# A two-layer conditioned decoder trunk on one core: two adaLN vectors moved from TensorE to VectorE rows, bf16 fillers spread through the norms, weight splits and a tanh pinned later

## The chip, the cores and the metric

The kernel runs on one NeuronCore of one Trainium2 chip. The metric is the device time of one execution in microseconds (us); several executions are timed and the median is given. Beside them stands one profiled execution, with its own time and the span from its first to its last instruction. PE is TensorE, DVE is VectorE, ACT is ScalarE, POOL is GpSimd, and SP is the queue from which all weight transfers are issued.

## The reference, cut to what matters

Two layers are computed on 256 tokens of width 1024, in float32. Each layer takes six vectors of 1024 from a conditioning vector `c`, which does not depend on the tokens:

```python
c_act = jax.nn.silu(c)
for l in range(DEPTH):
    # six vectors of layer l, r = 0..5
    sh1, sc1, g1, sh2, sc2, g2 = split(c_act @ w_mod[l] + b_mod[l], 6)
    h = modulate(rms_norm(x, mix_norm_g[l]), sh1, sc1)     # h*(1+sc)+sh
    x = x + g1 * token_mixer(h, ...)                       # MLA, MoBA, conv, gates, w_out
    h = modulate(rms_norm(x, ffn_norm_g[l]), sh2, sc2)
    x = x + g2 * channel_mixer(h, w_up[l], ..., w_down[l]) # conv over 3 tokens, silu(a)*b
```

Below, (l, r) is vector r of layer l: (0, 5) is the gain `g2` of layer 0, (1, 2) is `g1` of layer 1 and (1, 3) is `sh2` of layer 1. Each such vector needs a 1024 x 1024 matrix, 4 MB, that is read once.

## The kernel before, in words

Everything lies transposed: 128 partitions by 8 tiles of 256 tokens. Each large product is made of three float32r matmuls on halves of both operands (`flush`, L304 to L321): high by high, high by low, low by high. Weights come in units of 128x1024 float32 (512 KB). Each unit is loaded by SP (`wload_unit`, L218), then split into a high half by ACT (L232) and a low half by DVE (L233). `take` (L281) hands out the units in the order of use. It loads and splits up to three units beyond those asked for (`AHEAD` = 3), and four buffers of each kind rotate.

A planner of the compiler orders each engine's instructions by the order in which the program traces them and by when their operands are ready; an instruction that is ready early can stand well ahead of its place in the program. `tc.issue_after(i)` puts the instructions of its block that run on the engine of `i` behind `i`. After that each engine works its list in order.

The six vectors of each layer are made in one of two ways:

- as a part on TensorE (`mod_part`, L415 to L437): eight loads of 512 KB; for each, four matmuls with `c` as a 32-column stationary operand (L424, seen as eight records); then a copy, two transposes (L432) and an addition (L434);
- as rows on DVE (`mod_row`, `use_row`, L405 to L413): eight loads of 512 KB, each multiplied with `c` laid out along a row and summed in the same instruction (L407), then an addition of one column (L408).

Before, (0, 5) and (1, 3) are parts. They serve as filler in the two norms that stop the matmul stream: the norm ahead of the feed-forward block of layer 0 (called the first norm below), and the norm at the head of layer 1 (the second norm). There the eight residual updates (L1290, L1462) are followed by squares on ACT (L546), sums of pairs on DVE (L554), matmuls with a column of ones (L559), mean plus epsilon (L536), a power of -0.5 on POOL (L537), two transposes that spread the result (L569), and then eight tiles, each in three steps: L615 on DVE, L616 on ACT for the high half, L617 on DVE for the low half. The feed-forward or projection matmuls can begin with the first tile. `norm_stats` (L572) puts bf16 matmuls on constant ones (`warm`, L336) in between: 4, 7 and 3 of them.

Rows of (1, 0), (1, 1) and (1, 2) run during the feed-forward block of layer 0, those of (0, 3), (0, 4) and (1, 4) late in the two token mixers, and those of (1, 5) in the feed-forward block of layer 1. `c` is laid out as a row once more in each mixer: a load, a tanh on ACT (L1262) and a product on DVE (L1263).

The order of the mixers is written out by hand in `STEPS` (L76). In the late part, `G` are gate projections, `O` and `OC` output projections, `PR` the final projection, `RW0` to `RW3` make the row of `c`, and `r0`, `r1` mark the stretch over which rows are spread. The order of the feed-forward block comes from `_ffn` (L134): how many `up` steps run before the first `down` step. An `up` step is two units and its convolution (L1422 to L1433); `acts` are its high and low halves, the operands of `down`.

## Time and profile before

| | |
|---|---|
| median of 3 runs | 902.07 us (900.52 to 902.74) |
| profiled execution, its own time | 905.0 us |
| its span | 902.9 us |
| busy: PE, DVE, ACT, POOL | 881.3, 807.8, 556.9, 50.7 us |
| transfers | 201.59 MB, 223 GB/s in the mean |

In the rows of a timeline the first number is the start in us, the second the time in us until the last of the merged instructions ended, then engine, line, operation, out<-in with shapes, and how many instructions are merged; a bracket tells how long the engine had been idle and what ended that. A row of a group view has count, busy time and the mean of one in ns. A row of the windows view has a stretch, its length, and the busy time with count of PE, PEld (weight loads), DVE, ACT and POOL, then the granted clock, the share of busy DMA engines, and GB/s. Matmul ends are modelled: a float32r matmul of 256 columns shows 0.28 us but the next one starts 0.113 us after it.

### The profile page before, as it was taken

The page shows a single profiled execution, that of the slowest core. Times are in us where ns is not written, and L with a number is a line of the kernel's source. Part 1 is how long each engine was busy: PE and PEld are TensorE (multiplying, and loading weights), DVE is VectorE, ACT ScalarE, POOL GpSimd, SP SyncE. Part 2 cuts the span into 40 slices and gives each one's busy share as a digit, 9 for nine tenths or more (in the row PEclk, how much of TensorE's full clock was granted, in tenths as well). Part 3 has the DMA queues.
Part 4 walks back from the last instruction along what each step waited for, and adds up shares of the span by engine and source line. Part 5 has one row for each costly group of instructions (what it writes and reads, how often), then busy time and mean ns, then how long its engine had stood idle before and what let it go on. Part 6 is the DMA issues. An engine that isn't in the chain of part 4 may idle for free.

```text
span 902.9 us, 18611 instructions
## 1 busy us (share of the span) xinstructions
PE 881.3 (98%) x7247; PEld 836.2 (93%) x7247; DVE 807.8 (89%) x1592; ACT 556.9 (62%) x998; POOL 50.7 (6%) x36
## 2 busy tenths in 40 slices
PE   8999899999999999999999999999999999999998
PEld 6888788998997999999999988989999999999998
DVE  6989899999988999999875999999987899998774
ACT  4677579744666655556543676788465777556551
POOL 1010710000000000000000034000000000000000
PEclk8999999999999999999999999999999999999999
DMA  8956615598998989997752656157866575987631
GB/s 320 376 202 198 196 59 176 183 318 304 318 315 283 332 273 326 301 318 236 214 176 76 202 184 209 53 164 232 264 205 211 163 232 176 308 281 211 194 95 48
DMA packets 57976, 201.59 MB, mean 223 GB/s; under 512 B 6944, under 2 KB 8480, under 8 KB 57888
## 3 DMA queue, kind: packets, MB, share of 16 engines
q1 hardware_dynamic: 57888, 200.41, 66.9%
q8 instruction: 57, 0.93, 0.4%
q14 instruction: 31, 0.25, 0.1%
HBM read 199.33 MB, written 1.05 MB: 222 GB/s over the span
## 4 chain that ended last, share of the span: by engine, by line
PE 76%; DVE 13%; ACT 4%; DMA 4%; issue 2%; SPq 0%; POOL 0%; DVEq 0%; ACTq 0%; POOLq 0%
PE psb L316 15%; PE psb L317 15%; PE psb L319 15%; PE psa L316 7%; PE psa L317 7%; PE psa L319 7%; DVE wlo L233 4%; DVE cacc L1142 2%; ACT whi L232 2%; DVE raw L817 1%; PE psa L424 1%; PE psa L735 1%; PE psa L747 1%; PE psa L680 1%; DMA raw<-in_win 1%
## 5 line engine op out<-in xcount | busy, mean ns | idle before, releaser
L232 ACT ACTIVATE whi<-raw 128x1024 fp32r<-128x1024 f32 (+2 forms) x286 | 295.4, 1041 | 173.7 <-PE psb L317 90.7
L233 DVE TENSOR_TENSOR wlo<-raw,whi 128x1024 fp32r<-128x1024 f32 (+2 forms) x286 | 340.0, 1194 | 48.2 <-ACT whi L232 40.5
L316 PE MATMUL psb<-hh,whi 128*128 128x256 f32 x1056 | 254.7, 282 | 0.6 <-ACT p L714 0.3
L317 PE MATMUL psb<-hl,whi 128*128 128x256 f32 x1056 | 252.3, 279 | 0.0
L316 PEld LDWEIGHTS psb<-hh,whi 128*128 128x128 f32 x1056 | 198.6, 188 | 5.5 <-issue 3.3
L317 PEld LDWEIGHTS psb<-hl,whi 128*128 128x128 f32 x1056 | 198.8, 188 | 0.5 <-DVE wlo L233 0.4
L319 PE MATMUL psb<-hh,wlo 128*128 128x256 f32 x1056 | 144.2, 278 | 0.0
L319 PEld LDWEIGHTS psb<-hh,wlo 128*128 128x128 f32 x1056 | 131.0, 188 | 0.8 <-issue 0.8
L1142 DVE SCALAR_TENSOR_TENSOR cacc<-upad,cw,cacc 128x256 f32<-128x256 f32 x240 | 105.9, 479 | 0.4
L316 PE MATMUL psa<-mhl,whi 128*128 128x256 f32 x400 | 93.3, 277 | 0.0
L317 PE MATMUL psa<-mhl,whi 128*128 128x256 f32 x400 | 93.1, 276 | 0.0
L537 POOL TENSOR_TENSOR rs<-rs,mhalf 128x8 f32<-128x8 f32 (+3 forms) x26 | 49.1, 1900 | 674.4 <-DVE rs L536 674.4
L1424 DVE SCALAR_TENSOR_TENSOR e<-psb,fw,e 128x255 f32<-128x255 f32 (+1 forms) x168 | 79.8, 476 | 4.3 <-ACT e L1422 3.7
L316 PEld LDWEIGHTS psa<-mhl,whi 128*128 128x128 f32 x400 | 74.9, 188 | 0.0
L317 PEld LDWEIGHTS psa<-mhl,whi 128*128 128x128 f32 x400 | 74.9, 188 | 0.0
L1422 ACT ACTIVATE e<-psb,fb,fw 128x256 f32<-128x256 f32 x84 | 46.5, 554 | 37.3 <-DVE e L1424 34.7
L407 DVE SCALAR_TENSOR_TENSOR raw<-raw,crow 128x1024 f32<-128x1024 f32 x56 | 68.1, 1215 | 0.0
L319 PE MATMUL psa<-mhl,wlo 128*128 128x256 f32 x400 | 53.5, 276 | 0.0
L319 PEld LDWEIGHTS psa<-mhl,wlo 128*128 128x128 f32 x400 | 49.1, 188 | 0.0
L1432 ACT ACTIVATE mhl<-e 128x256 fp32r<-128x256 f32 x44 | 18.4, 417 | 43.6 <-DVE e L1430 42.1
L316 PE MATMUL psb<-whi,hh 128*128 128x416 f32 (+1 forms) x96 | 30.8, 349 | 3.2 <-ACT hh L893 3.1
L317 PE MATMUL psb<-whi,hl 128*128 128x416 f32 (+1 forms) x96 | 29.6, 343 | 0.2 <-DVE hl L894 0.2
(295 smaller groups left out, 1522.9 us busy)
## 6 DMA issues: line engine op xcount, KB each, us to landing
raw<-in_wup SPq DMA_DIRECT2D x88, 512.0 KB, 4.9
raw<-in_wmr SPq DMA_DIRECT2D x68, 512.0 KB, 5.4
raw<-in_wdn SPq DMA_DIRECT2D x44, 512.0 KB, 4.6
raw<-in_wgab SPq DMA_DIRECT2D x32, 512.0 KB, 4.9
raw<-in_wqkv SPq DMA_DIRECT2D x24, 512.0 KB, 4.8
raw<-in_wm SPq DMA_DIRECT2D x24, 512.0 KB, 4.4
raw<-in_win SPq DMA_DIRECT2D x16, 512.0 KB, 4.5
raw<-in_wgc SPq DMA_DIRECT2D x16, 512.0 KB, 4.1
```

The costliest lines, as they stand in the source:

```text
L232: ac.activation(hi, raw, AF.Copy)
L233: ve.tensor_tensor(lo, raw, hi.bitcast(F32), op=ALU.subtract)
L316: te.matmul(o, p1[0], p1[1], start=start, stop=False)
L317: te.matmul(o, p2[0], p2[1], start=False, stop=False)
L319: last = te.matmul(o, p3[0], p3[1], start=False, stop=stop)
L407: ve.scalar_tensor_tensor(raw, raw, scale, row, op0=ALU.mult, op1=ALU.mult, accum_out=acc)
L424: te.matmul(acc[32 * c:32 * c + 32, 0:S], cact[:, k:k + 1].to_broadcast([P, 32]), raw[:, c * S:(c + 1) * S], start=(k == 0), stop=(k == KD ...
L537: gp.tensor_tensor(r, r, mhalf[:, :n], op=ALU.pow)
L1142: ve.scalar_tensor_tensor(aj, upad[:, j, t:t + S], cw[:, j * 31 + t:j * 31 + t + 1], aj, op0=ALU.mult, op1=ALU.add)
L1422: ac.activation(t, src, AF.Identity, scale=fw[:, 2, c:c + 1], bias=fb[:, c:c + 1])
L1424: ve.scalar_tensor_tensor(t[:, d:S], src[:, 0:S - d], fw[:, 2 - d, c:c + 1], t[:, d:S], op0=ALU.mult, op1=ALU.add)
L1432: ac.activation(mh, th, AF.Copy)
```

## The change

- (0, 5) and (1, 3) are no longer parts on TensorE but rows on DVE. Their rows and those of (1, 2) are placed anew: 27 rows in the feed-forward block of layer 0 ((1, 0), (1, 1), (0, 5) and three of (1, 2)), one for each `up` step from the third on and two from the 13th to the 19th, each behind the low half of two `up` steps earlier; eight rows in the input projection of layer 1 (five of (1, 2), three of (1, 3)), behind the last tile; and the last five rows of (1, 3) in the late mixer of layer 1, in a new stretch `r2` to `r3`. The stretch `r0` to `r1` of (1, 4) ends earlier.
- The two norms have 5, 3, 9 and 7 bf16 fillers, placed ahead of the third and of the fourth pair of ones-matmuls, behind the fourth, and behind the transposes.
- The last unit taken before each of these norms is loaded but not split. It is split behind the last square (ACT) and behind the low half of the fourth tile (first norm) or of the third (second norm). In the input projection of layer 1 tiles are traced three ahead, and each split stands behind the newest tile. The instructions of the first two `up` steps of layer 0 stand behind the eighth tile (`MARK` = 7), where it was the second.
- The tanh that makes the row of `c` stands behind the last attention's high output half (L750).
- In layer 0 four `up` steps come before the first `down` step, where it was three.

```diff
-F1 = 2
-MARK = 1
+MARK = 7
+LATER = 1
+TWO_ROWS = range(12, 19)
+GATE_ROWS = {4: [(2, 3), (2, 4)], 5: [(2, 5), (2, 6)], 6: [(2, 7), (3, 0)], 7: [(3, 1), (3, 2)]}
-WARM1 = (4, 7, 3)
+WARM1 = (5, 3, 9, 7)
-ROWS = [(0, 0), (0, 1), (1, 0), (1, 1), (1, 2), (1, 5)] + RPARTS
+ROWS = [(0, 0), (0, 1), (0, 5), (1, 0), (1, 1), (1, 2), (1, 3), (1, 5)] + RPARTS
...
-    "OC0 G70 OC1 PR0 OC2 OC3 PR1 OC4 OC5 G71 O6 O7 PR2 OC6 PR3 OC7 PR4 r1 PR5 PR6 PR7 "
+    "r1 OC0 G70 OC1 r2 PR0 OC2 OC3 PR1 OC4 OC5 G71 O6 O7 r3 PR2 OC6 PR3 OC7 PR4 PR5 PR6 PR7 "
...
-FFN = [_ffn(2, 3), _ffn(4, 4)]
+FFN = [_ffn(3, 3), _ffn(4, 4)]
...
+    def split_rest(keep=0):
+        while len(raws_in) > keep:
+            raw, lead, ks = raws_in.pop(0)
+            ready.append((split(raw, lead), raw.shape[1] // len(ks), ks))
...
-            ready.append((split(wload_unit(src), lead), src.shape[1] // len(ks), ks))
+            raws_in.append((wload_unit(src), lead, ks))
+            split_rest(later[0])
...
-    def norm_stats(fill=None):
-
-        step(fill or iter(()), F1)
-        bank = psb() if sum(WARM1) else None
+    def norm_stats():
+
+        bank = psb()
...
-        if fill:
-            with tc.issue_after(last.ins):
-                step(fill, KD - F1)
...
+    def split_behind(mark):
+        hold[0] = [squares[0].ins, mark.ins]
+        split_rest()
+        hold[0] = None
...
+            with ExitStack() as es:
+                if n == 8 and k > 3:
+                    with tc.issue_after(last.ins):
+                        es.enter_context(tc.issue_after(warm(bank, WARM1[k // 2 - 2]).ins))
+                elif n == 8:
+                    es.enter_context(tc.issue_after((last if k > 1 else newest[0]).ins))
...
-        fill = mod_part(1, 3, ("oal", "obl", "vb", "lh0", "lh1", "lh2")) if l == 1 else None
...
         for k in range(KD):
             if l > 0:
-                norm_tile(k, bc, gs1[:, k:k + 1], sh1[:, k:k + 1], hh, hl)
+                if k + 3 < KD:
+                    tile(k + 3)
+                hold[0] = [i.ins for i in tiles[-1]]
                 conv_in(k)
-                mod_row(crow1[0], l, 2, k, scale=0.5 if CDMA else 1.0)
+                hold[0] = None
+                for n, (r, i) in enumerate(GATE_ROWS.get(k, ())):
+                    with tc.issue_after(tiles[-1][1].ins):
+                        mod_row(crow1[0], l, r, i, (SPARE[2 * (k % 2) + n], 1), 0.5 if CDMA else 1.0)
...
-                ac.activation(th, crow1[0], AF.Tanh, scale=0.5)
+                with tc.issue_after(heads[0].ins):
+                    ac.activation(th, crow1[0], AF.Tanh, scale=0.5)
...
-            fill = mod_part(l, 5)
-            bc = norm_stats(fill)
+            bc = norm_stats()
             hh, hl = new_h()
-            marks = [norm_tile(k, bc, gs2[:, k:k + 1], mod[l][:, 24 + k:25 + k], hh, hl) for k in range(KD)]
+            for k in range(KD):
+                marks.append(norm_tile(k, bc, gs2[:, k:k + 1], mod[l][:, 24 + k:25 + k], hh, hl))
+                if k == 3:
+                    split_behind(marks[k][1])
...
-        rows_left = [(1, r, k) for r in ((5,) if l else range(2)) for k in range(KD)]
+        rows_left = [(n, r, k) for n, r in (((1, 5),) if l else ((1, 0), (1, 1), (0, 5))) for k in range(KD)]
+        rows_left += [] if l else [(1, 2, k) for k in range(3)]
...
-                mod_row(crow1[0], *rows_left.pop(0), scale=0.5 if CDMA else 1.0)
+                row_next()
+                if not l and j in TWO_ROWS:
+                    row_next()
...
+        def row_next():
+            with tc.issue_after(parts[-3].ins):
+                mod_row(crow1[0], *rows_left.pop(0), scale=0.5 if CDMA else 1.0)
```

More of the change, by code (lines that the diff above doesn't have):

```diff
@@ L293, in take1 @@
         return take()[0][0][1]
-    queue = []
+    queue, newest = [], [None]
     def mmw(o, w, v, start, stop):
@@ L311, in flush @@
                 te.matmul(o, p2[0], p2[1], start=False, stop=False)
-                te.matmul(o, p3[0], p3[1], start=False, stop=stop)
+                newest[0] = te.matmul(o, p3[0], p3[1], start=False, stop=stop)
             queue.clear()
-            return None
+            return newest[0]
         for o, p1, p2, _, start, _ in queue:
@@ L552, in sq_sums @@
                 continue
-            else:
-                ve.tensor_tensor(one, one, sq, op=ALU.add)
-                if SQ4 and n == 4 and k < 3:
-                    continue
-            with tc.issue_after(warm(bank, WARM1[0]).ins) if bank is not None and WARM1[0] and k == n - 1 else ExitStack():
+            ve.tensor_tensor(one, one, sq, op=ALU.add)
+            if n == 4 and k < 3:
+                continue
+            with ExitStack() as es:
[4 more added lines that the diff above has]
+                    es.enter_context(tc.issue_after((last if k > 1 else newest[0]).ins))
                 for b in range(NB):
                     last = te.matmul(st[:, b:b + 1], one[:, b * P:(b + 1) * P], ones,
-                                     start=(k == (3 if SQ4 and n == 4 else 1) and b == 0),
-                                     stop=(k == n - 1 and b == 1))
+                                     start=(k == (3 if n == 4 else 1) and b == 0), stop=(k == n - 1 and b == 1))
         return st[:, 0:NB], last
@@ L907, in layer @@
             hold[0] = None
-        step(fill or iter(()))
         ahead[0] = AHEAD
@@ L1229, in project @@
                 acc.extend(psa() for _ in range(4))
+            if j == KD - 2 and l == 0:
+                later[0] = LATER
             if j % 2 == 0:
                 wor[:] = [u[0][1] for u in take(2)]
+            later[0] = 0
             for n in range(KD):
@@ L1307, in layer @@
         gs2 = mod_gain(l, 4, "ffn_g")
-        pre, marks, fill = [], [], None
+        pre, marks = [], []
         if l == 0:
@@ L1388, in down @@
                 acc2.extend(psa() for _ in range(4))
+            if j == NF - 1:
+                later[0] = LATER
             w = take1()
+            later[0] = 0
             for n in range(KD):
@@ L1455, in layer @@
                 up(j)
-            if j == 1 and fill:
-                step(fill)
         raw_tags[:] = [("raw", 4)]
```

43 lines of the change are left out of this document (26 added, 17 removed).

## The prediction

> **What bounds the kernel now.** I read the page first, then PE's timeline around the two norms, then the windows view for DVE's free time, then the rows of the tanh. The page's first part says who is full.
>
> ```profile
> span 902.9 us, 18611 instructions
> PE 881.3 (98%) x7247; PEld 836.2 (93%) x7247; DVE 807.8 (89%) x1592; ACT 556.9 (62%) x998; POOL 50.7 (6%) x36
> ```
>
> PE is busy almost throughout, so time is won only where PE is busy with something that is not needed, or pauses. One such place is the first norm. PE's timeline there:
>
> ```profile
> 277.63 0.28 PE L311 MATMUL psa<-mhl,whi 128*128 128x256 f32 x1
> 277.74 0.28 PE L312 MATMUL psa<-mhl,wlo 128*128 128x256 f32 x1
> ...
> 282.80 0.43 PE L569 MATMUL psb<-ident,rs 128*128 128x128 f32 x2 [0.31 <-POOL rs L537]
> ...
> 283.49 1.93 PE L424 MATMUL psa<-raw,cact 128*32 128x256 f32 x32
> 285.35 0.38 PE L316 MATMUL psb<-hh,whi 128*128 128x256 f32 x1
> ...
> 287.77 0.64 PE L424 MATMUL psa<-raw,cact 128*32 128x256 f32 x8
> 289.56 0.64 PE L424 MATMUL psa<-raw,cact 128*32 128x256 f32 x8
> ```
>
> The first two rows give the pace of useful work: one matmul every 0.113 us (to two digits 0.11), a unit of 24 in 2.72 us. The projection's last one starts at 277.74, the feed-forward block's first at 285.35, 7.6 us later, and fill (L424) stands ahead of it and twice inside the block that follows. What the block had done by 292.30, shown by the windows view for writers of the tile `psb` alone:
>
> ```profile
> 285.30:292.30 7.00, 5.81 (x46) 1.00 0.86 301
> ```
>
> It had 46 matmuls. The chain that brings the first tile runs over DVE and ACT (DVE's rows, then ACT's):
>
> ```profile
> 278.46 1.22 DVE L233 TENSOR_TENSOR wlo<-raw,whi 128x1024 fp32r<-128x1024 f32 x1
> 279.59 0.48 DVE L1290 SCALAR_TENSOR_TENSOR x<-psa,g1h,x 128x256 f32<-128x256 f32 x1
> 283.26 1.26 DVE L615 SCALAR_TENSOR_TENSOR e<-x,gs,psb 128x256 f32<-128x256 f32 x3 [1.37 <-PE psb L569]
> 283.78 0.91 ACT L616 ACTIVATE hh<-e,mod 128x256 fp32r<-128x256 f32 x2 [3.20 <-DVE e L615]
> ```
>
> A weight split stands ahead of the last residual update, whose operand PE had finished at 277.74 + 0.28 = 278.02. It holds the chain up by 279.59 - 278.46 = 1.13 us. The second norm has the same form (PE, DVE, then one ACT row):
>
> ```profile
> 468.15 0.28 PE L312 MATMUL psa<-mhl,wlo 128*128 128x256 f32 x1
> 473.46 2.80 PE L424 MATMUL psa<-raw,cact 128*32 128x256 f32 x48
> 476.19 0.38 PE L316 MATMUL psa<-hh,whi 128*128 128x256 f32 x1
> 469.25 1.22 DVE L233 TENSOR_TENSOR wlo<-raw,whi 128x1024 fp32r<-128x1024 f32 x1
> 470.39 0.42 DVE L554 TENSOR_TENSOR e<-e,e 128x256 f32<-128x256 f32 x1
> 473.24 1.26 DVE L615 SCALAR_TENSOR_TENSOR e<-x,gs,psb 128x256 f32<-128x256 f32 x3 [1.40 <-PE psb L569]
> 474.43 1.27 DVE L617 SCALAR_TENSOR_TENSOR hl<-e,mod,hh 128x256 fp32r<-128x256 f32 x3
> 468.98 0.87 ACT L546 ACTIVATE e<-x 128x256 f32<-128x256 f32 x2 [0.21 <-DVE x L1462]
> ```
>
> PE could have begun with the first low half at 474.43 + 0.42 = 474.85, but fill held it until 476.19.
>
> **The change part by part.** The sum is made against the profiled execution, 905.0 us with its span of 902.9; the median of the three runs is 902.07, and I carry the difference over to it unchanged.
>
> *First norm.* Without the split the chain is 1.13 us earlier: L615 starts at 282.13, the first high half is ready about 0.95 us after that (283.78 - 283.26 and one of the two ACT tiles), and PE can start near 283.1. Then tiles set the pace: by L615 (1.26 for three) and L617 (1.27 for three) a tile takes DVE about 0.8 us, eight take 6.6, and with the one held split (1.13) and the four small tap copies (some 0.4) the last low half is there near 290.3. Three units, 8.2 us of work, are at hand meanwhile, since the third is split behind the fourth tile. Dense from 284.1 on, they would be done by 292.3: 72 matmuls where the rows show 46, 26 x 0.113 = 2.95 us ahead. I take 2.4, since PE needs more than the first four tiles only late, but surely waits some 0.5 us for tiles in the first unit. The bounds are 1.1 (only the split goes; the tiles hold PE afterwards) and 2.95. Holding the first two steps behind the eighth tile costs nothing as long as the three units last: the next high half can be made by 291.3, and PE asks for it at 292.3. If a tile is late by more than that 1 us, PE waits.
>
> *Second norm.* The last sum waits for the split until 470.39; its square is ready at 468.98 + 0.87 = 469.85, so 0.5 us goes. Without fill PE starts its stream at 474.85 instead of 476.41 (one matmul after 476.19), another 1.56. Together 2.1; here a unit needs one tile only, 2.72 us of PE against 0.8 of DVE, so tiles do not hold PE. Bounds: 0.5, and 0.5 + 2.73 (473.46 to 476.19) = 3.2, were all of the fill in the way. The fillers that replace it, 9 behind the last pair of ones-matmuls (1.0 us) and 7 behind the transposes (0.8), fit into the waits there: from 282.80 + 0.43 to the first tile is just about 1 us.
>
> *The rest of the parts.* Each part has two transposes in the middle of the stream later:
>
> ```profile
> L432 PE MATMUL psa<-ident,e x6: 270/273/328, 254.8 to 498.5; 128*128 128x128 f32 x6
> L424 PE MATMUL psa<-raw,cact 128*32 128x256 f32 x192 | 14.5, 386 | 0.1
> L407 DVE SCALAR_TENSOR_TENSOR raw<-raw,crow 128x1024 f32<-128x1024 f32 x56 | 68.1, 1215 | 0.0
> ```
>
> Four of these six go: between 0.4 (0.11 each) and 1.1 us (0.27 each); I take 0.5. Of the 192 fill records 128 go, but their PE time lies in the two norms and is counted there.
>
> *The rows.* Sixteen rows are new. A row is 1.215 us and 0.08 for reading the sum and adding the column: 1.29, so 20.6 us of DVE. The loads stay sixteen of 512 KB on SP, since a row takes the place of a part's load; where a row's load waits for its buffer, weight loads queue behind it on SP. None of this lies on PE's path if DVE and the queue have room where it is put. Room is read from the windows view (the fifth column is DVE):
>
> ```profile
> 350.00:415.00 65.00, 65.00 (x575) 65.00 (x574) 65.00 (x126) 35.45 (x54) 0.00 (x0) 1.00 0.92 312
> 476.00:500.00 24.00, 24.00 (x211) 23.81 (x204) 11.25 (x20) 9.73 (x17) 0.00 (x0) 1.00 0.31 87
> 580.00:600.00 20.00, 19.68 (x190) 18.41 (x186) 20.00 (x40) 16.39 (x40) 0.00 (x0) 1.00 0.34 107
> 660.00:680.00 20.00, 20.00 (x179) 20.00 (x178) 17.13 (x30) 14.82 (x25) 0.00 (x0) 1.00 0.66 209
> 680.00:700.00 20.00, 20.00 (x178) 20.00 (x178) 15.59 (x27) 11.55 (x19) 0.00 (x0) 1.00 0.63 202
> ```
>
> In layer 0's feed-forward block DVE is full from 350 to 415, where two rows run for each `up` and `down`, and yet PE does not pause: 65.00 of 65.00. Afterwards 27 rows stand there instead of 24, but over all steps, and at most two for each step, for seven steps. Their transfers, 0.92 of the engines' time in that window, also stay at two for each step. Cost 0. The first four `up` steps in a row with a row in two of them may cost a little; I put 0.3 (0 to 1). The eight rows in the input projection need 10.3 us of the 12.75 that DVE has free from 476 to 500. What spills over delays the stretch behind it, where DVE is full (580 to 600). I put 0.3 (0 to 3). Their transfers come at a time when the DMA engines are a third busy (0.31): 0. The five in the late mixer need 6.5 of the 7.3 us that are free from 660 to 700. Queued behind such a row stand a split or the halves of a merged tile, and the projection on PE waits for those. The three units of reserve hide one row, not two in succession: 0.8 (0 to 6.5, all of them).
>
> *The tanh.* In layer 1 it stands ahead of the last attention's exponentials on ACT (L714), whose bias (L701) is done earlier; the rows below are ACT's, DVE's and PE's:
>
> ```profile
> 610.61 1.06 ACT L1262 ACTIVATE th<-crow 128x1024 f32<-128x1024 f32 x1
> 612.04 0.47 ACT L714 ACTIVATE p<-psa,nb,rs 128x128 f32<-128x128 f32 x1
> 627.52 1.06 ACT L232 ACTIVATE whi<-raw 128x1024 fp32r<-128x1024 f32 x1 [2.89 <-PE psb L317]
> 611.51 0.16 DVE L701 SCALAR_TENSOR_TENSOR nb<-mx,rs 128x4 f32<-128x4 f32 x1
> 635.35 0.67 PE L1155 MATMUL psb<-e,mean_w 128*128 128x256 f32 x2 [0.50 <-DVE mod L408]
> ```
>
> The exponentials could start 612.04 - 611.67 = 0.4 us earlier. The product and the first row follow the tanh to behind the attention, which frees 2.5 us of a full DVE; PE's pause of 0.5 us at the convolution's mean (635.35) may go. Behind the attention the 1.06 us of the tanh stand ahead of weight splits on ACT, but there ACT was idle for 2.89 us (627.52): 0. Together at most 1.0, and nothing if PE's other work fills these gaps anyway; I take 0.5. In layer 0 I put nothing.
>
> Sum: -2.4 - 2.1 - 0.5 - 0.5 + 0.3 + 0.3 + 0.8 = -4.1 us. The profiled execution goes from 905.0 to 900.9, the median from 902.07 to 898.0. 0.3% of the median is 2.7 us, about what a measurement of this kernel can tell from no change: faster means under 899.4, slower over 904.8.
>
> **The rivals.** *The gain is half taken back.* PE's starts move as forecast, but the first norm gives only its lower bound (1.1), as tiles hold PE, and the late rows cost two and a half of five (3.2): -1.1 - 2.1 - 1.0 + 0.6 + 3.2 = -0.4, 901.7, no change. For it: the first unit needs four tiles, 3.3 us of DVE, for 2.72 us of PE. Against it: two units can use these four tiles.
>
> *DVE becomes the bound of layer 1.* Thirteen new rows, 16.8 us, go into a layer where DVE is full at 580 to 600 and PE loses time. The two holes together have 12.75 + 7.3 = 20 us. If only a third can be used, since a row stands in the queue ahead of what PE needs, 16.8 - 6.7 = 10.1 us come onto the path: with -5.5 from the terms other than rows, and the 0.3 of layer 0, that is +4.9, 907.0, slower. It decides from the point on where less than 8.9 us of the holes serve (-5.5 + 0.3 + 7.9 = +2.7, and 16.8 - 7.9 = 8.9). Against it: the rows of the input projection stand where PE reads units split well ahead, and the planner puts unpinned rows into DVE's gaps.
>
> *The clock falls.* The granted clock is 1.00 in all windows above, that from 285.30 behind the first norm among them; the longest pause of PE in that norm shows as 0.31 us idle (282.80). With the fill gone, 24 fillers of 0.113 are 2.7 us of a norm of some 5.5; pauses of up to 1 us come back ahead of the last pairs. Were the clock to be halved over the first unit, each of its 24 matmuls would cost 0.113 more: 2.7 for each norm, 5.4 in all, 903.4, no change. The Trainium skill, "TensorE: Matmul & The Clock Gate", Part 1, says that the array falls back to half clock after an idle window of about 3.4 us; by that rule it does not happen here, and the trace agrees so far as a pause of 0.31 us left the clock at 1.00.
>
> *The change does not do what it says:* `issue_after` orders, it does not reserve. If the planner fills DVE's or ACT's queue in the norm with something else (a row, a step's convolution), both norms keep 1 us less each: -2.1, 900.0, no change.
>
> **How the numbers follow.** Forecast 0.60; half taken back 0.16; other work in the norms 0.08; the clock 0.03; DVE as the bound 0.13. So faster 0.60, no change 0.27, slower 0.13. The best sum takes every bound in favour: -2.95 - 3.2 - 1.1 - 1.0 = -8.2, 893.9; I start the range at 894.0. At the other end it takes in the cases of no change up to 903.5. Outside lie the 0.13 of the slower case and a few hundredths of the clock's.
>
> **What would show it.** Right: L316 starts some 5.5 us after the last L312 of the first norm, where it was 7.6, and some 6.0 after that of the second, where it was 8.0; no L233 between L1290 or L1462 and L536; from 290 to 460 no pause on PE; rows L407 right behind the last L617 of layer 1, done before the next stretch's convolution. Wrong: PE waits for L233 or L617 for over 1 us after the eighth tile; pauses at the projection of layer 1 that end with `mhl`; a granted clock under 1.00 behind a norm.

## The result and the profile after

The changed kernel takes 908.57 us (median of 6 runs, 906.48 to 910.27), the kernel before, on the same chip, 901.3 us (6 runs, 899.75 to 902.74). The ratio is 1.0079, with a 95% interval of 1.0058 to 1.0100: slower by 7 us, where I had forecast 4.1 us faster.

The profiled execution of after took 908.17 us, with a span of 906.0. That is only 3.1 above the span of before that the prediction quotes, and this number is not to be trusted: the profiled execution of before had an accident. Its rows, from PE's and POOL's timelines:

```profile
93.86 9.44 POOL L537 TENSOR_TENSOR rs<-rs,mhalf 128x16 f32<-128x16 f32 x2 [0.24 <-DVE rs L536]
106.95 0.28 PE L317 MATMUL psb<-hl,whi 128*128 128x256 f32 x1
110.30 2.08 PE L678 MATMUL psa<-qkT 96*128 96x128 f32 x8 [3.08 <-ACT qkT L1124]
```

Two powers on POOL took 9.44 us there. before_again is a second profile of the same kernel.

> The kernel before, unchanged, for a second profile. If the pause of 3.35 us at 106.7 and the slow matmuls behind it belonged to that one execution alone, they are gone and the span is near 897 us; if they are the kernel's ordinary course, they are there again and the span is near 903; half as much would say that the timed executions differ among themselves in this.

Four such powers take 10.60 us there, PE does not pause (the windows view has it busy for 23.86 of 24 us from 100 to 124), and the span is 897.5:

```profile
89.76 10.60 POOL L537 TENSOR_TENSOR rs<-rs,mhalf 128x16 f32<-128x16 f32 x4 [21.34 <-DVE rs L536]
```

From here on every kernel is laid against before_again. After is 906.0 - 897.5 = 8.5 us longer, which fits the 7.3 of the medians. The page's first part and the chain of after:

```profile
span 906.0 us, 18397 instructions
PE 876.4 (97%) x7135; PEld 835.9 (92%) x7135; DVE 827.9 (91%) x1638; ACT 557.1 (61%) x996; POOL 48.6 (5%) x36
PE 51%; DVE 30%; DMA 8%; ACT 5%; issue 5%; SPq 0%; POOL 0%; DVEq 0%; ACTq 0%; POOLq 0%
```

DVE has 20 us more to do (827.9 against 807.8), and the chain that ended last now runs over DVE and transfers for 38% of the span (before: 13% and 4%).

Where was it lost? All kernels of this study have the same 6264 large-product matmuls (`flush`), so the start of the n-th one can be compared between two traces. The table gives, stretch by stretch (times as in the profile of before), how much more time than before_again a kernel needed; the last column of stretches ends with the start of the last of these matmuls, so the sum is the difference of the spans to 0.1 us (0.3 to 0.4 below it in norms_only, norms_free and sixteen_out). I worked it out from the starts of all these matmuls.

| kernel | to 278 | first norm, to 300 | 300-400 | 400-468 | second norm, to 495 | 495-530 | 530-606 | 606-650 | 650-700 | to end | sum |
|---|---|---|---|---|---|---|---|---|---|---|---|
| after | +0.7 | -3.0 | 0.0 | +6.3 | -2.3 | +1.6 | +1.5 | -1.2 | +4.5 | +0.4 | +8.5 |
| first_two | +0.4 | -3.0 | +1.3 | +1.2 | -2.4 | +1.1 | +1.7 | -1.2 | +4.2 | +0.4 | +3.6 |
| first_four | +0.8 | -3.3 | -0.5 | +3.9 | -2.4 | +1.2 | +1.6 | -1.0 | +2.9 | -0.6 | +2.6 |
| old_splits | -0.7 | -1.6 | -0.5 | +6.5 | -2.4 | +4.3 | +1.7 | -1.2 | +5.4 | 0.0 | +11.5 |
| taps_first | +0.8 | -3.3 | +4.1 | +0.5 | -2.4 | +1.6 | +1.6 | -1.0 | +4.3 | -0.8 | +5.4 |
| late_out | +1.1 | -3.0 | 0.0 | +8.0 | -2.4 | +1.3 | +1.6 | -1.0 | 0.0 | -0.3 | +5.2 |
| tanh_free | +1.0 | -3.0 | 0.0 | +7.7 | -2.4 | +1.5 | +2.0 | -1.0 | +2.6 | -0.6 | +7.8 |
| late_later | +0.9 | -3.0 | 0.0 | +8.4 | -2.4 | +0.9 | +1.6 | -1.2 | +3.8 | -0.5 | +8.4 |
| norms_only | +0.7 | -3.0 | +1.0 | -0.1 | -2.3 | -0.3 | +1.7 | -0.8 | +1.6 | +0.4 | -1.1 |
| norms_free | -1.0 | -2.9 | +1.6 | -0.1 | -1.8 | -0.3 | +3.0 | -0.6 | +1.2 | -0.5 | -1.6 |
| norm2_new | -0.1 | -3.0 | +0.9 | -0.1 | -2.3 | +1.1 | +1.5 | -1.2 | +0.3 | +0.3 | -2.5 |
| part13 | +1.5 | -3.0 | +1.3 | 0.0 | +0.1 | 0.0 | 0.0 | -1.2 | 0.0 | -0.6 | -1.9 |
| early_rows | -0.3 | -3.3 | +15.5 | +2.1 | -2.4 | +1.5 | +1.6 | -1.0 | +3.9 | -0.4 | +17.2 |
| early_tags | +0.3 | -3.0 | +14.0 | +0.9 | -2.4 | +0.8 | +1.6 | -1.0 | +2.8 | +0.6 | +14.7 |
| early_two | +1.1 | -3.0 | +14.8 | +0.3 | -2.3 | +0.7 | +1.6 | -1.0 | +3.3 | -0.3 | +15.2 |
| early_old | +0.1 | -2.0 | +7.8 | +1.0 | -2.4 | +3.5 | +1.6 | -1.0 | +4.4 | -0.4 | +12.5 |
| early_free | +7.0 | -1.0 | -0.1 | +0.1 | -2.4 | +3.4 | +1.6 | -1.2 | +2.5 | +0.6 | +10.6 |
| sixteen_out | +1.4 | -3.3 | +9.2 | +0.6 | -2.4 | -0.3 | +3.1 | -0.8 | 0.0 | -0.5 | +6.9 |

Each row is one execution. late_out, tanh_free and late_later were altered in layer 1 alone, and yet have 7.7 to 8.4 us at 400 to 468 where after has 6.3; differences of up to 2 us in that column can be chance.

The first row tells the story. Both norms gain what was forecast (-3.0 and -2.3 against -2.4 and -2.1). PE's timeline of after, the last product of a block and the first of the next, in the first norm and in the second:

```profile
272.18 0.28 PE L322 MATMUL psa<-mhl,wlo 128*128 128x256 f32 x1
...
277.70 0.50 PE L326 MATMUL psb<-hh,whi 128*128 128x256 f32 x2 [0.35 <-ACT hh L630]
...
466.07 0.28 PE L322 MATMUL psa<-mhl,wlo 128*128 128x256 f32 x1
...
471.57 0.62 PE L326 MATMUL psa<-hh,whi 128*128 128x256 f32 x3 [0.35 <-ACT hh L630]
```

5.5 us each, where it was 7.6 and 8.0. Then 6.3 us are lost at the end of layer 0's feed-forward block, and some 7 in layer 1. The end of the block on PE:

```profile
451.67 0.28 PE L322 MATMUL psa<-mhl,wlo 128*128 128x256 f32 x1
454.27 0.38 PE L320 MATMUL psa<-mhl,whi 128*128 128x256 f32 x1 [2.32 <-ACT mhl L1467]
454.73 0.40 PE L321 MATMUL psa<-mhl,whi 128*128 128x256 f32 x1
454.95 0.39 PE L322 MATMUL psa<-mhl,wlo 128*128 128x256 f32 x1
...
457.27 0.41 PE L321 MATMUL psa<-mhl,whi 128*128 128x256 f32 x1
460.17 0.38 PE L320 MATMUL psa<-mhl,whi 128*128 128x256 f32 x1 [2.48 <-ACT mhl L1467]
460.39 0.28 PE L322 MATMUL psa<-mhl,wlo 128*128 128x256 f32 x1
```

The last two `down` steps wait for the halves of the last two `up` steps. Between the two pauses a matmul comes every 0.21 us instead of every 0.113; the windows view from 451 to 462 has a granted clock of 0.84. The pauses cost 2.60 - 0.11 and 2.90 - 0.11 from start to start, the slow matmuls some 1.5 (13 steps from 454.27 to 457.27 in 3.00 us, less 13 x 0.113). That is 6.8 together; the table has 6.3, and before_again itself waits 0.2 us there.

Why are these halves late, in a block in which PE had not paused before? DVE's share from 290 to 335, first after, then before_again (fifth column DVE):

```profile
290.00:335.00 45.00, 45.00 (x392) 45.00 (x392) 38.85 (x76) 25.50 (x41) 0.00 (x0) 1.00 0.76 248
```

```profile
290.00:335.00 45.00, 45.00 (x394) 44.84 (x394) 44.15 (x87) 28.59 (x44) 0.00 (x0) 1.00 0.91 305
```

DVE idles 6.15 us in after, 0.85 in before_again. From 335 to 450 it is busy for 113.7 of 115 us in after, so it has 1.3 us left there to win them back. What it waits for in after from 290 to 345, and what ACT waits for there (columns: us in total, times, longest):

```profile
DVE mhl L1468 <- ACT mhl L1467: 3.4, 2, 1.9
DVE e L1459 <- ACT e L1457: 2.7, 2, 2.0
```

```profile
ACT whi L236 <- DMA raw<-in_wup: 11.7, 5, 3.5
```

The same wait in before_again:

```profile
ACT whi L232 <- DMA raw<-in_wup: 3.2, 2, 2.7
```

One of these places in the timeline of after, ACT's and DVE's rows:

```profile
312.50 1.07 ACT L236 ACTIVATE whi<-raw 128x1024 fp32r<-128x1024 f32 x1 [1.61 <-DMA raw<-in_wdn]
...
315.49 1.07 ACT L236 ACTIVATE whi<-raw 128x1024 fp32r<-128x1024 f32 x1 [1.92 <-DMA raw<-in_wup]
316.45 0.55 ACT L1457 ACTIVATE e<-psb,fb,fw 128x256 f32<-128x256 f32 x1
...
317.04 0.48 DVE L1459 SCALAR_TENSOR_TENSOR e<-psb,fw,e 128x255 f32<-128x255 f32 x1 [2.00 <-ACT e L1457]
```

L1457 is here the first tap of one of the two convolutions of the fifth `up` step. Its product was complete before 310, but in ACT's list it stands behind two weight splits, and both wait for their transfer. DVE waits for the tap.

And why do weights come late? SP's timeline after the start of the block, first after (block starts at 277.70), then before_again (279.10):

```profile
281.86 0.33 SPq L209 DMA_DIRECT2D raw<-in_wup  x1
284.62 0.33 SPq L399 DMA_DIRECT2D col<-in_cols  x1
286.14 1.46 SPq L209 DMA_DIRECT2D raw<-in_wup  x2
```

```profile
283.86 0.33 SPq L205 DMA_DIRECT2D raw<-in_wup  x1
284.23 1.19 SPq L389 DMA_DIRECT2D col<-in_cols  x1
286.18 0.33 SPq L205 DMA_DIRECT2D raw<-in_wup  x1
```

Two units of the block had been loaded before 243 us in either kernel. With them, in order of issue, eight had been issued by the start of the block in after, the ninth came 4.2 us after it and the tenth 8.4. In before_again nine had been issued by the start, and the tenth came 4.8 us after it. So the norm became 2.1 us shorter for PE, and the tenth unit stands 3.7 us later against what PE needs. The other 1.6 us are a later load: the tenth unit is issued 14.0 us after the projection's last matmul in after, 12.4 in before_again, and 12.8 in old_splits, where this norm holds no split. SP's waits for low halves from 255 to 345 show why, first after, then before (the last column is the longest):

```profile
SPq L209 <- DVE wlo L237: 48.4, 24, 13.3
```

```profile
SPq L205 <- DVE wlo L233: 28.6, 22, 2.3
```

In after the held unit is split behind the fourth tile, and SP stands for 13.3 us until its buffer is free.

### The profile page after: what moved, and what is told of

It reads as the page before. It is cut to its first block, busy times and chain, and to the rows that moved or that the text cites. A ratio compares the mean times of both kernels' runs of the same rounds, so it can differ in the third digit from the quotient of the medians.

```text
span 906.0 us, 18397 instructions
## 1 busy us (share of the span) xinstructions
PE 876.4 (97%) x7135; PEld 835.9 (92%) x7135; DVE 827.9 (91%) x1638; ACT 557.1 (61%) x996; POOL 48.6 (5%) x36
## 4 chain that ended last, share of the span: by engine, by line
PE 51%; DVE 30%; DMA 8%; ACT 5%; issue 5%; SPq 0%; POOL 0%; DVEq 0%; ACTq 0%; POOLq 0%
DVE wlo L237 10%; PE psb L326 9%; PE psb L327 9%; PE psb L329 8%; PE psa L329 6%; PE psa L327 5%; PE psa L326 5%; DVE raw L417 5%; DVE cacc L1167 3%; DVE e L1459 3%; DMA raw<-in_wup 3%; ACT whi L236 2%; DMA raw<-in_wgab 1%; DVE raw L830 1%; DMA raw<-in_wmr 1%
## 5 line engine op out<-in xcount | busy, mean ns | idle before, releaser
L237 DVE TENSOR_TENSOR wlo<-raw,whi 128x1024 fp32r<-128x1024 f32 (+2 forms) x286 | 339.3, 1193 | 26.6 <-ACT whi L236 26.0
L417 DVE SCALAR_TENSOR_TENSOR raw<-raw,crow 128x1024 f32<-128x1024 f32 x72 | 87.2, 1219 | 2.1 <-DMA raw<-in_wmr 2.1
L547 POOL TENSOR_TENSOR rs<-rs,mhalf 128x8 f32<-128x8 f32 (+3 forms) x26 | 47.0, 1822 | 678.6 <-DVE rs L546 677.1
L1457 ACT ACTIVATE e<-psb,fb,fw 128x256 f32<-128x256 f32 x84 | 46.6, 554 | 38.5 <-DVE e L1459 35.3
L326 PE MATMUL psa<-hh,whi 128*128 128x256 f32 x128 | 29.5, 279 | 0.4 <-ACT hh L630 0.4
```

The lines of the kernel that those rows point to most:

```text
L237: ve.tensor_tensor(lo, raw, hi.bitcast(F32), op=ALU.subtract)
L326: te.matmul(o, p1[0], p1[1], start=start, stop=False)
L417: ve.scalar_tensor_tensor(raw, raw, scale, row, op0=ALU.mult, op1=ALU.mult, accum_out=acc)
L547: gp.tensor_tensor(r, r, mhalf[:, :n], op=ALU.pow)
L1457: ac.activation(t, src, AF.Identity, scale=fw[:, 2, c:c + 1], bias=fb[:, c:c + 1])
```

## The experiments

Seventeen kernels were run, besides the second profile of the kernel before. Ratios are to the kernel before on the same chip; the changed kernel has 1.0079.

**early_rows.** First theory: DVE carries a debt to the end because rows run up to the last step. So they were placed earlier.

```diff
-TWO_ROWS = range(12, 19)
+TWO_ROWS = range(2, 13)
```

> The changed kernel with one constant altered: two rows for each of the 3rd to 13th up steps instead of the 13th to 19th, so that the 27 rows of layer 0's feed-forward block are placed behind the 3rd to 18th step and the last four steps have none. Nothing is left out. Theory of the debt (DVE carries its backlog to the end of the block because rows run up to its last step, and the last down steps wait for the halves of the last up steps): the two pauses of 2.6 and 2.9 us near 451 to 460 us and the slow matmuls between them go, about 6 us: 902.5 us. Rival, four up steps in a row set the lag: the pauses stay within 1 us, 907.5 to 908.6. Rival, the pauses only move forward, to where the rows are now dense (PE waits for mhl near 350 to 420): between 904 and 910 with pauses there.

918.63 us, ratio 1.0178 (1.0157 to 1.0199). The pauses at the end go, as the theory said, but PE waits for low halves of weights (L237) from 309 to 398 instead, and 300 to 400 takes 15.5 us more. The last rival had the pauses move forward, as they did, but named `mhl` as what PE waits for, and was far too mild in size.

**first_two.** Three `up` steps first, as before.

```diff
-FFN = [_ffn(3, 3), _ffn(4, 4)]
+FFN = [_ffn(2, 3), _ffn(4, 4)]
```

(and the two entries of `LEADS` for up step 4 back to 3.)

> The changed kernel with three up steps ahead of the first down step in layer 0, as in the kernel before, instead of four; all rows stay where the change put them. Theory of the debt: DVE's backlog is set by its own work, not by PE's order, so the lag at the end is the same to 1 us and the pauses stay: 907.5 to 909.5 us; with one step less of reserve PE may pause earlier too, up to 911. Rival, four in a row cost the 6 us: 902 to 903.

903.69 us, ratio 1.0030 (1.0010 to 1.0050); the twelve executions spread from 901.5 to 908.6. The theory of a debt from DVE's own work fell: 27 rows in the same places, and 5 us less in the median. The fourth step in a row carries most of the loss in this block.

**late_out.** The five rows of (1, 3) in the late mixer are not computed.

```diff
-        o = _spread(o, [("R", 3, k) for k in range(3, KD)], ("r", 2), ("r", 3))
...
+    ve.memset(mod[1][:, 27:32], 0.0)
```

> The changed kernel without the last five rows of (1, 3): their loads, products and additions in the late mixer of layer 1 are left out and the five columns are set to zero (this part of the computation is changed). Theory that these rows hold up PE there: PE's pauses of 1.95 and 1.27 us at 656 and 665 us go and the late mixer of layer 1 is 3 to 5 us shorter: 903.5 to 905.5 us. Rival, the tanh behind the attention and the shorter stretch for (1, 4) did it: at most 1.5 us shorter, 907 or more.

904.48 us, ratio 1.0027 (1.0012 to 1.0041): 4.1 us less, and the table has 0.0 instead of +4.5 at 650 to 700. Shown: five rows of 1.22 us, 6.1 us of DVE, cost PE 4 to 4.5 us there. In after, DVE's row and what stands behind it (DVE, POOL, PE):

```profile
655.33 1.22 DVE L417 SCALAR_TENSOR_TENSOR raw<-raw,crow 128x1024 f32<-128x1024 f32 x1 [1.16 <-DMA raw<-in_wmr]
...
657.16 0.15 DVE L546 TENSOR_SCALAR rs<-psb 128x2 f32<-128x2 f32 x1
...
657.46 0.80 POOL L547 TENSOR_TENSOR rs<-rs,mhalf 128x2 f32<-128x2 f32 x1 [97.29 <-DVE rs L546]
...
658.31 0.43 PE L582 MATMUL psb<-ident,rs 128*128 128x128 f32 x2 [1.68 <-POOL rs L547]
```

DVE waits 1.16 us for the row's transfer and then computes it for 1.22; the statistics of the convolution's norm (L546) stand behind it, and PE waits for them.

**sixteen_out.** All sixteen rows out, those of (1, 2) in layer 0 with two a step for the 3rd to 10th step.

```diff
-TWO_ROWS = range(12, 19)
+TWO_ROWS = range(2, 10)
-GATE_ROWS = {4: [(2, 3), (2, 4)], 5: [(2, 5), (2, 6)], 6: [(2, 7), (3, 0)], 7: [(3, 1), (3, 2)]}
+GATE_ROWS = {}
...
+    ve.memset(mod[0][:, 40:48], 0.0)
+    ve.memset(mod[1][:, 24:32], 0.0)
```

> The changed kernel without all sixteen rows of (0, 5) and (1, 3), whose columns are set to zero (this part of the computation is left out); the rows of (1, 2) are all in layer 0's feed-forward block, as in the kernel before, 24 there, ended by the 18th up step. The norms' fillers, held splits, the late tanh and four up steps in a row stay. Theory that the norms gain what was forecast and the rows give it back: 901.3 - 3.0 - 2.3 and up to 1 for the rest = 895 to 897 us, with no pause over 1 us behind either norm. Rival, the new form of the norms costs later (held splits, the mark on the eighth tile): 900 or more.

907.61 us, ratio 1.0059 (1.0038 to 1.0079). This test was badly made: with 24 rows early it has the illness of early_rows (+9.2 at 300 to 400), so it says nothing of the norms. norms_only repeats it.

**old_splits.** Second theory: the held splits starve SP in the norm.

```diff
-MARK = 7
+MARK = 1
-            if j == KD - 2 and l == 0:
-                later[0] = LATER
```

> The changed kernel with the weight splits around the first norm as before: the last unit ahead of it is split when it arrives, and the first two up steps stand behind the second tile instead of the eighth. Four up steps in a row and all rows stay. Theory of the supply (the held splits keep the weight buffers full through the first norm, SP issues one load in 13 us there, the weights then arrive late from 290 to 335 us, ACT waits for them with the first tap behind it, DVE idles 6 us that it never wins back, and PE pays them at the end of the block): the idle time of DVE from 290 to 335 falls from 6.2 to under 3 us, the pauses at 451 to 460 shrink by 3 us or more, the norm gives back about 1: 905 to 907 us. Rival, four up steps in a row are the cause by themselves (they bring the tap of the fifth step behind a split that waits): idle time and pauses stay, 908.5 to 910.

909.43 us, ratio 1.0072 (1.0043 to 1.0101), no gain. DVE's idle time from 290 to 335 falls to 4.0 us and PE's wait at the end from 4.8 to 3.6, but slow matmuls follow a pause of 3.64 us, the norm gives back 1.4, and the block is no shorter. This execution also lost 2.8 us more than after at 495 to 530, behind a second long pause. The held splits alone are not the cause.

**early_tags.** early_rows with the rows' loads over four buffers.

```diff
-                mod_row(crow1[0], *rows_left.pop(0), scale=0.5 if CDMA else 1.0)
+                turn_row[0] += 1
+                mod_row(crow1[0], *rows_left.pop(0), (SPARE[turn_row[0] % 4], 1), 0.5 if CDMA else 1.0)
```

> The kernel with the rows behind the 3rd to 18th up step (918.6 us), with the rows' loads going round over four buffers instead of two by two. Theory that a row's load waits on SP for the buffer of the row two ahead, and the weight loads queued behind it come late: SP's waits for L417 (32 us from 255 to 460) all but go, PE's pauses of 13 us in the block go, 905 us or less. Rival, two more transfers for each step ahead of the weights are too many while no reserve is left, whatever the buffers: 916 to 919.

917.61 us, ratio 1.0183 (1.0145 to 1.0220). The four buffers did not shorten SP's waits for rows (L417): 30.9 us from 255 to 460, 30.7 in early_rows. So the time did not change, and what these waits cost is not shown.

**tanh_free.** The tanh without its pin.

```diff
-                with tc.issue_after(heads[0].ins):
-                    ac.activation(th, crow1[0], AF.Tanh, scale=0.5)
+                ac.activation(th, crow1[0], AF.Tanh, scale=0.5)
```

> The changed kernel with the tanh not pinned behind the last attention, as before. Theory that the pin delays the rows of (1, 4) by 15 us (first one at 632 instead of 617) and so presses thirteen rows into 44 us: they start near 620 again, the pauses at 656 and 665 us shrink by half or more, and the time falls by 1 to 3 us: 905.5 to 907.5. Rival, the five rows are too many there in any place: within 0.8 us of the changed kernel, 908 to 909.5.

910.07 us, ratio 1.0094 (1.0066 to 1.0121). The first row of (1, 4) starts at 616 again, the second only at 634, and the loss at 650 to 700 falls from 4.5 to 2.6, but the time does not follow: other stretches of this execution take more (the block's end +7.7). The pin makes no difference to the time that these runs can tell.

**late_later.** The marks `r2` and `r3` moved to PR2 and PR7.

> The changed kernel with the stretch of the last five rows of (1, 3) moved from around the first output projections to PR2 up to PR7, where DVE had 6.5 us free from 682 to 706. Theory that the place costs, not the rows: the pauses at 656 and 665 go and none comes at the last projections, 904.5 to 906 us. Rival, the five rows cost the same anywhere in the late mixer, since what DVE does late there holds up the merged halves that PE needs: 907.5 to 910 us.

908.00 us, ratio 1.0073 (1.0047 to 1.0098). The expectation was not tested: the planner pulls the rows forward to where their data are ready. The five start between 656 and 676 us, in after between 655 and 675. A place in the program's text is no place on the engine.

**norms_only.** first_two, without the sixteen rows; 24 rows in the block (`TWO_ROWS = range(12, 16)`), the same columns set to zero.

> The changed kernel with three up steps ahead of the first down step and without the sixteen rows of (0, 5) and (1, 3), whose columns are set to zero (this part of the computation is left out). 24 rows in layer 0's feed-forward block, one a step and two for the 13th to 16th step, none in layer 1's input projection, eight in its late mixer. It holds what the change does to the norms, and the late tanh. Theory that the norms gain 3.0 and 2.3 us and that four up steps in a row and the rows give it back: 895 to 897.5 us, and no pause of about 2 us near 511 and 600, if the rows of the input projection make those. Rival, the norms' gain is taken back downstream whatever the rows are (weights late behind the first norm, the pauses near 511 and 600): 899 us or more.

898.68 us, ratio 0.9965 (0.9950 to 0.9981): 3 us faster than before, where 4 to 6 were expected. The norms' 5.3 are all there in the table; 3.3 come back at 530 to 606 and 650 to 700, with none of the moved rows in place.

**part13.** A combination of what the runs pointed to: first_two, (1, 3) a part in the old second norm, 24 rows in the block, the eight rows of (1, 2) in the input projection, none of (1, 3) as rows.

```diff
-FFN = [_ffn(3, 3), _ffn(4, 4)]
+FFN = [_ffn(2, 3), _ffn(4, 4)]
-TWO_ROWS = range(12, 19)
+TWO_ROWS = range(12, 16)
-GATE_ROWS = {4: [(2, 3), (2, 4)], 5: [(2, 5), (2, 6)], 6: [(2, 7), (3, 0)], 7: [(3, 1), (3, 2)]}
+GATE_ROWS = {4: [(2, 0), (2, 1)], 5: [(2, 2), (2, 3)], 6: [(2, 4), (2, 5)], 7: [(2, 6), (2, 7)]}
...
-            bc = norm_stats()
+            bc = norm_old(fill)
```

> A combination, nothing left out: the changed kernel with three up steps ahead of the first down step, (1, 3) again a part on TensorE in a second norm as before, (0, 5) as rows in the feed-forward block (24 rows there), the eight rows of (1, 2) in layer 1's input projection, none of (1, 3) in the late mixer. Theory that the first norm's 3.0 us stay and the eight rows in the input projection cost at most 2: 898 to 900.5 us, faster than both kernels or as fast as the one before. Rival, the rows in the input projection cost as much as they did in the late mixer, 1 us each and more: 903 or more.

897.50 us, ratio 0.9964 (0.9944 to 0.9984): faster than both kernels. Its span is 895.6 us. DVE from 290 to 335:

```profile
290.00:335.00 45.00, 43.70 (x380) 43.50 (x380) 43.42 (x83) 27.80 (x43) 0.00 (x0) 1.00 0.80 263
```

DVE idles 1.6 us, and PE waits 0.2 us at the block's end. Layer 1 loses nothing from 480 to 606, though eight rows stand in its input projection as in after. Here they start between 471.4 and 486.6 us, the first 1.4 us after the projection's first matmul; in after between 483.4 and 495.5, the first 11.8 us after it. The second norm ahead of them is another one too, so this run alone does not say which of the two helps.

**first_four.** Five `up` steps first (`_ffn(4, 3)`).

> The changed kernel with five up steps ahead of the first down step in layer 0 instead of four; nothing left out. Theory of the lead (each further up step in a row puts PE another step ahead of DVE, which stands full for the rest of the block and cannot shorten it, and the lead is given back in pauses when the up steps run out): 3 to 5 us more than the changed kernel, 911.5 to 913.5, with longer pauses at 451 to 463 us or new ones at the first down steps. Rival, four in a row were an unlucky order of one split and one tap on ACT: five may fall either way, 903 to 909.

902.64 us, ratio 1.0012 (0.9996 to 1.0027). The theory of the lead fell too: one step more costs 6 us less. What goes with the loss, roughly, is not the number of steps but the idle time of DVE from 290 to 335. By kernel, DVE's idle time there (45 less the busy time) and PE's wait at the end of the block for the halves:

| | idle, us | wait, us | rows in the block |
|---|---|---|---|
| late_out | 6.4 | 6.4 | 27 |
| after | 6.2 | 4.8 | 27 |
| old_splits | 4.0 | 3.6 | 27 |
| first_four | 1.5 | 2.6 | 27 |
| first_two | 1.5 | 1.5 | 27 |
| part13 | 1.6 | 0.2 | 24 |
| before_again | 0.9 | 0.2 | 24 |

In first_two and part13 PE had already waited 1.3 us for halves before 300, which this wait does not contain. And late weights are not enough for the loss: in first_two, first_four, part13 and norms_only, too, the tenth unit is issued 8.4 to 8.5 us after the block's start, and ACT waits for transfers from 290 to 345 for 8.6, 12.2, 9.7 and 9.1 us (13.5 in after, 3.2 in before_again). Yet from 300 to 468 the table has 2.5, 3.4, 1.3 and 0.9 us there, against 6.3 in after.

**taps_first.** Four steps in a row; the units loaded in steps 4 to 7 are split behind that step's first taps.

```diff
+            late_split = not l and 3 <= j < 7
+            if late_split:
+                later[0] = 2
...
+            if late_split:
+                hold[0] = [taps1[-1].ins]
+                split_rest()
```

> The changed kernel, four up steps in a row, nothing left out; only in the 4th to 7th up step of layer 0 the two units loaded there are split behind that step's first taps on ACT instead of ahead of them. Theory of the blocked tap (on ACT a tap whose operand is ready stands behind splits that wait for their weights; DVE idles 6.2 us from 290 to 335, never wins it back, and PE pays it at the end of the block): the idle time of DVE there falls to under 3 us, the pauses at 451 to 460 from 5.5 to 2.5 us or less, 904 to 906 us. Rival, the order on ACT is only the sign of weights that come too late: DVE then waits for the splits instead, the idle time stays near 6 us, 907.5 to 910.

906.88 us, ratio 1.0081 (1.0060 to 1.0101), no gain by the ratio. The idle time falls to 3.5 us and the wait at the end to 0.6, as the theory said; but now PE itself waits, from 300 to 335, where it did not in after:

```profile
PE psb L326 <- ACT whi L236: 2.9, 4, 1.4
```

With what else it lost there, 300 to 400 takes 4.1 us more. So the tap behind a waiting split is how the loss reaches the block's end. The new pauses are not late weights: ACT waits for transfers from 290 to 345 for only 1.9 us here, where it was 13.5, but the splits now stand behind taps, and PE waits for the splits.

**norms_free.** norms_only without the pins on layer 1's splits.

```diff
-                hold[0] = [i.ins for i in tiles[-1]]
                 conv_in(k)
-                hold[0] = None
```

(and without holding the last unit ahead of the second norm.)

> The kernel with the norms' changes and without the sixteen rows (898.7 us), and now also without the pins of layer 1's splits: the last unit ahead of the second norm is split when it comes, and the splits in the input projection do not stand behind the newest tile. The sixteen rows' columns are zero (this part of the computation is left out). Theory that these pins upset the order of the work behind them (1.8 us at 570 to 606 and 1.6 at 650 to 700): both go, 895 to 897 us, less up to 1 that the second norm gives back. Rival, the order behind is changed by anything: the losses turn up elsewhere, 898 to 900.

899.09 us, ratio 0.9983 (0.9972 to 0.9994). The losses in layer 1 stay (3.0 and 1.2): the pins do not make them.

**norm2_new.** part13 with the change's second norm, (1, 3) left out.

> The combination that was fastest (three up steps first, 24 rows in layer 0's feed-forward block with (0, 5) among them, the eight rows of (1, 2) in layer 1's input projection), but with the change's second norm, and with (1, 3) left out: its column is zero and neither its part nor its rows are there (this part of the computation is left out). Theory that the new second norm starts the projection 2.3 us sooner and the work behind gives it back, because DVE is full from 504 to 617 and its order there is another: 897 to 899 us, with 1.5 to 3 us lost at 570 to 606. Rival, the loss in the earlier kernels came with the rows of the late mixer or with (1, 2) in layer 0: 895 to 896, and nothing lost there.

898.37 us, ratio 0.9975 (0.9963 to 0.9987). 2.3 us are gained at the second norm, 1.1 and 1.5 lost at 495 to 530 and 530 to 606, where part13 loses nothing. The 1.5 go with the new norm: norms_only, without rows in the projection, has 1.7 there. The 1.1 need the rows as well: norms_only has -0.3, and the rows start 11.8 us after the projection's first matmul here, as in after. Both pauses are in after. The first, in DVE's rows of after:

```profile
512.15 2.85 DVE L1167 SCALAR_TENSOR_TENSOR cacc<-upad,cw,cacc 128x256 f32<-128x256 f32 x7
514.92 0.23 DVE L546 TENSOR_SCALAR rs<-lss 128x3 f32<-128x3 f32 x2
515.06 0.47 DVE L1167 SCALAR_TENSOR_TENSOR cacc<-upad,cw,cacc 128x256 f32<-128x256 f32 x1
515.46 1.26 DVE L975 SCALAR_TENSOR_TENSOR qll<-psb,col,qlh 128x256 fp32r<-128x256 f32 x3
```

PE waits 1.8 us for L975, ahead of which the planner has put eight taps of the mixer's convolution. DVE has no room here (from 495 to 530 it is busy for 34.0 of 35 us in after, 34.9 in before_again). When the projection ahead ends sooner, PE arrives sooner at work that DVE has not done; that this is the reason is argued, not tested.

**early_two, early_old, early_free.** Why do early rows cost 15 us, when the kernel before runs two a step there for nothing? early_two is early_rows with three steps first; early_old is that with the old splits; early_free is early_two without the pin on the rows.

> The changed kernel with three up steps ahead of the first down step and with two rows for each of the 3rd to 13th up step; nothing left out. Theory that early rows cost where no weights are in reserve behind the first norm, which four up steps in a row make worse: the block loses 5 us or less against the 17 of the kernel with early rows, and its end has no pause: 904 to 908 us. Rival, two rows a step ahead of the weights on SP are too many in any order behind this norm: 911 to 915.

> Three up steps first, two rows for each of the 3rd to 13th step (916.1 us), and the weight splits around the first norm as before it: the last unit is split when it comes, the first two steps stand behind the second tile. Nothing is left out. Theory of the reserve (behind the new norm no weights are in reserve, so that every load that waits behind two rows' loads on SP is late): the block up to 400 us loses 5 us or less where it lost 15, and the time is 906 to 908 us. Rival, the reserve is not it: 10 or more are lost again, 914 to 918.

> The same kernel with early rows (916.1 us), splits as the change has them, but no row is pinned behind the low half of two steps earlier: the planner may place it anywhere, as in the kernel before. Nothing is left out. Theory of the pins (a pinned row comes late on DVE, its buffer comes free late, and the next row's load stands on SP ahead of weights until then): the block loses 5 us or less, 904 to 907 us. Rival, the pins are not it: 10 or more are lost again, 914 to 918.

916.09 us (1.0168; 1.0153 to 1.0184), 911.56 us (1.0119; 1.0102 to 1.0137) and 908.38 us (1.0073; 1.0054 to 1.0093). Four in a row has little part in it; the old splits give back half (+7.8 instead of +14.8 at 300 to 400). Without pins the block loses nothing, but then eight rows run from 257 to 293 us, seven of them ahead of the block, and 7.0 us are lost up to 278. PE's wait in early_two from 300 to 400 shows what it is:

```profile
PE psa L329 <- DVE wlo L237: 8.5, 3, 3.6
```

A unit is loaded into a buffer that DVE frees with a low half. With DVE behind and no unit in reserve, loads, splits and DVE would wait for one another in a ring, and PE for the ring; SP's 58.6 us of waits for L237 from 285 to 400 (40.9 in before_again) fit this, and no run tests it alone. How much of the other half is due to the pins and how much to the eight rows that moved out of the way is not separated.

## Why the prediction was wrong

*First norm, -2.4:* -3.0 in nearly every kernel that has it. Right, at its bound of 2.95; PE starts 5.5 us after the projection, as forecast.

*Second norm, -2.1:* -2.3 measured, right; but I took it to stay won. Against part13, norm2_new loses 2.6 behind it: 1.5 with the norm alone, 1.1 only where eight rows stand in the projection too.

*The rows in layer 0's block, "Cost 0", and four steps in a row, 0.3 (0 to 1):* this is the step that failed: 6.3 measured at the block's end, of which some 5 go with the fourth `up` step in a row (first_two). I had read the windows view, "DVE is full from 350 to 415 ... and yet PE does not pause", as room. It says the opposite: an engine that is full for the rest of the block can win back nothing that it loses at its head. Two things ran up that debt: 5.3 us more idle time of DVE at 290 to 335, where taps stood on ACT behind splits that waited for their weights; and three rows more, 3.9 us of DVE, by which first_two waits 1.3 us longer at the end than part13 at the same idle time. My own sign, "from 290 to 460 no pause on PE", looked at the right place; my sum ended the block at 415.

*Left out altogether:* that weights are loaded during the norm. I counted the shorter norm as a gain for PE and asked only whether the three units at hand would last; the rate at which the next ones come I did not look up, though SP's timeline of before had it. Nor did I ask what a held unit does to its buffer: SP stood 13.3 us for it. Without the fourth step in a row and without new rows this costs little: norms_only has 1.0 us at 300 to 400.

*Late rows, 0.8 (0 to 6.5):* 4.1 by late_out. The mechanism, a row ahead of what PE needs, was named and its size taken near the wrong end.

*Rows in the input projection, 0.3 (0 to 3):* about 1.6 in after (495 to 530: +1.6 with them, -0.3 without in norms_only), nothing in part13. There they stand 10 us earlier against the projection, and behind the old norm; which of the two decides is not separated.

*Tanh, -0.5:* no difference that can be told. *Transposes, -0.5:* not measured alone.

*The rivals.* "DVE becomes the bound of layer 1", 907.0, came nearest, for half a reason: layer 1 gives back some 6.4 us (1.6 + 1.5 - 1.2 + 4.5), which the mechanism covers in part (the 1.5 come without any new row), but the larger single loss is in layer 0, for which it had 0.3. That its 907.0 lies near the 908.57 is luck. The clock behind the norms stayed at 1.00, as forecast; it fell at the block's end, where I expected no pause.

*What stays open:* why four steps in a row bring taps behind waiting splits more than three or five do; where 1.5 to 3.0 us come from at 530 to 606 with the new second norm; and 1.2 to 1.6 at 650 to 700 in norms_only and norms_free without late rows. The planner's order differs in all of them.

## What to carry to other kernels

An engine that is full without anyone waiting for it is not free for more: follow its lag to the end of the stage, where the others run out of work ahead and the lag is paid. A pause of the matmul engine may be the time in which weights are loaded; before shortening it, count the units that are issued in it, and how late the next ones will be. Where a moved piece of work runs is read in the trace: eight rows cost 1.4 us at one place (norm2_new against norms_only, 495 to 530) and nothing in part13, where they ran 10 us earlier in the projection, behind another norm.

## What the hardware showed that I had not expected

The matmul rate halved after pauses shorter than I thought safe, and not after some longer ones. In after it fell to one in 0.21 us behind an idle time of 2.32 us, and was full again behind the next one, of 2.48 us (rows above). In late_later it fell to one in 0.21 us 0.8 us after an idle time of 2.02 us (at 454.13). In sixteen_out an idle time of 3.25 us left it at one in 0.12:

```profile
342.38 1.19 PE L327 MATMUL psa<-mhl,wlo 128*128 128x256 f32 x8 [3.25 <-DVE wlo L235]
343.41 0.28 PE L324 MATMUL psb<-hh,whi 128*128 128x256 f32 x1
343.53 0.28 PE L325 MATMUL psb<-hl,whi 128*128 128x256 f32 x1
```

So between 2.0 and 3.3 us it is open which comes in these runs. The Trainium skill, "TensorE: Matmul & The Clock Gate", Part 1, gives an idle window of about 3.4 us for the fall; the 2.32 us of after do not agree with that as a threshold on a single pause, and the measurement decides. And one power on POOL can hold up the whole kernel: in one execution two of them took 9.44 us, one alone 7.84, where four took 10.60 in another; DVE waited 2.8 us for it, and up to 278 us PE lost 6.2.
